# A two-layer diffusion backbone on one core: which engine prepares the operands of the ConvFFN's down projection

## The chip, the core and the metric

The kernel runs on one core of a Trainium2 chip. The core has a matrix engine (TensorE, PE in the profile, with its weight loads as PEld), VectorE (DVE), ScalarE (ACT), GpSimd (POOL) and SyncE (SP), which issues nearly all transfers. Each engine works through its own queue of instructions in order, and semaphores hold an instruction until what it needs is there. The metric is the time of one execution on the device in microseconds; smaller is better.

## What is computed

Two layers act on 1024 latent tokens and 256 context tokens of width 1024. Layer 0 mixes by a Fourier transform and a gated linear attention, layer 1 by grouped-query attention. Each layer ends in a ConvFFN, and the change lies in the last matrix product of these two:

```python
def conv_ffn(h, w_up, w_conv, b_conv, w_down):
    u = dwconv_centred(h @ w_up, w_conv, b_conv)
    g, v = jnp.split(u, 2, axis=-1)
    return (jax.nn.silu(g) * v) @ w_down
...
    h_lat = h_lat + ga2 * conv_ffn(f_lat, w_ffn_up[i], w_ffn_conv[i], b_ffn_conv[i], w_ffn_down[i])
```

The inner width is 2816. Layer 0 puts all 1280 tokens through it, layer 1 the 1024 latent tokens. All is float32.

## The kernel before

**Three products for one.** A float32 operand is split (L206): ScalarE rounds it to the matrix engine's short form (`hi`, the CAST rows of L208), and a subtraction gives the remainder (`lo`, rows of L204). `mm3` then sums lo·hi, hi·lo and hi·hi in PSUM. The subtraction needs `hi`, so it waits for ScalarE. It runs on VectorE, unless another engine is passed in. A row of L204 is thus any two-operand instruction of the helper `tt`: the remainder of a split, a sum or a difference.

**Seven products for eight.** The up and the down projection use a Strassen-like scheme. The weight matrix and the token matrix are cut into 2 by 2 blocks (A11 to A22, B11 to B22), and seven products of block sums give the result. `DOWN` (L1350) lists those of the down projection in their order; the page's rows show them as the matmuls of L154, 128x320 wide in layer 0 and mostly 128x512 wide in layer 1. One product is made of four groups `r` of 128 output columns; a group takes 11 tiles `f` of 128 inner rows, so 33 matmuls for each PSUM bank.

**Weights.** `down_w` (L1424) is a generator that fetches the weight block of product `i`, group `r`, in three pieces of 4, 4 and 3 tiles, that is 512, 512 and 384 columns. Four of the seven products (S1, S3, S2, S4) need a sum of two blocks: two transfers, then a sum in place (L1443) on GpSimd. That makes 48 sums per layer, 32 of 128x512 and 16 of 128x384. The sums S1 and S2 are also stored to DRAM (`sd`, L1454) and loaded again as operands of S2 and S4. Each piece is then split; the table `WE` (L1459) names the engine of the remainder for the three pieces: GpSimd for all three in layer 0, and VectorE, GpSimd, VectorE in layer 1. The pieces lie in ten slots `W`; the generator goes on when a slot is free.

**Tokens.** The class `Ys` (L1359) loads the activations `y` from DRAM in pairs of tiles, forms the block differences that the second, third, fourth and sixth product need (`SUMS`, rows of 128x1280 or 128x1024), and splits each tile `f` of each product `i` (128x640 in layer 0, 128x512 in layer 1). The table `YE` (L1355) names the engine of the remainder: GpSimd for one `f` in three, VectorE for the others. `TE` (L1356) names VectorE for every block difference. A tile's slot `S` is freed when the last group of its product has used it, so most tiles of the next product are made while the last group runs.

**Results.** Each group's PSUM result is added to the residual by VectorE (`resid`, L918), partly by way of L204 rows that read PSUM.

**What sets the order.** The matrix engine's order is written out by hand in both ConvFFNs (L1721, L2052). The order on the other engines is chosen when the kernel is built, by a scheduler that follows the order of the program text and its own estimate of times; `order(first, then)` pins one instruction behind another. In `Ys.conv` a block difference is pinned behind the last split if both are on the same engine.

Of the kernel before, what the change touches and what calls it, by code (L numbers as in the profile page):

```python
# [15 lines left out]
ALU = mybir.AluOpType  # L16
# [88 lines left out]
def tile_hybrid_dit(  # L105
# [12 lines left out]
    V = nc.vector  # L118
    A = nc.scalar
    G = nc.gpsimd  # L120
# [82 lines left out]
    def tt(out_, a, b, op, eng=None):  # L203
        return (eng or V).tensor_tensor(out_, a, b, op)  # L204

    def split(src, hi, lo, eng=None):  # L206

        A.copy(hi, src)  # L208
        return tt(lo, src, hi.bitcast(F32), ALU.subtract, eng)
# [100 lines left out]
    def order(first, then):  # L310

        tc.add_manual_dep(then.ins, first.ins.name, mybir.DependencyInfo(
            mybir.DependencyClass.NoSync, mybir.DependencyReason.DATA), reason="order of the engine")
# [319 lines left out]
    def gla_gates(hf):  # L633

        la = []
        wg = gw[:32, 0, :].rearrange("r (d c) -> r d c", d=2)
        for ct in range(2):
            ab = GM((NT, 256))
            mn = GM((NT, 256))
            for t0, t1 in ((0, 4), (4, 5)):  # L640
                ps = banks(GB, 1024, 2)
                for t in range(t0, t1):
                    c0 = hf * HALF + t * P
                    PE.matmul(ps[:, (t - t0) * 256:(t - t0 + 1) * 256], z_all[:32, c0:c0 + P],
                              wg[:, :, ct * P:(ct + 1) * P], start=True, stop=True)
                pv = ps[:, :(t1 - t0) * 256].rearrange("p (t c) -> p t c", c=256)
                A.activation(ab[:, t0:t1, :], pv, AF.Abs)
                V.tensor_scalar_min(mn[:, t0:t1, :], pv, 0.0)
            A.activation(ab.a, ab.a, AF.Exp, scale=-1.0)
            la.append((ab, mn))  # L650
        for ab, mn in la:
            A.activation(ab.a, ab.a, AF.Ln, bias=1.0)
            tt(ab.a, mn.a, ab.a, ALU.subtract)
            mn.free()
        b = []
        for ct in range(2):
            ab = la[ct][0]
            b.append(GM((2, HALF)))
            for d in range(2):
                ps = banks(GB, HALF, 2)  # L660
                for t in range(NT):
                    PE.matmul(ps[:, t * P:(t + 1) * P], ab[:, t, d * P:(d + 1) * P], gm[:, 7 + d, :],
                              start=True, stop=True)
                A.copy(b[ct][:, d, :], ps)  # L664
            ab.free()
        return b
# [320 lines left out]
    with stream(6):  # L987
        ta, tr = AM(1280), AM(1280)
        R = ta[:, 1024:1280][:, 0:192].rearrange("p (m v b) -> p m v b", m=3, v=2)
# [46 lines left out]
    with stream(1):  # L1036
        b = gla_gates(0)
# [3 lines left out]
    with stream(1):  # L1041
        b = gla_gates(1)
# [309 lines left out]
    KF = NF // 2  # L1352
    LEAVE = (4, 4, 4, 5, 2, 2, 0)
    AHEAD = 3
    YE = ((V, V, G),) * 3 + ((V, G, V),) * 4  # L1355
    TE = (V, V, V, V, V, V, V)  # L1356
    SUMS = {1: ("B11", "B12", "B11"), 2: ("B12", "B22", "B12"), 3: ("B11", "B22", "B11"), 5: ("B11", "B21", "B11")}

    class Ys:  # L1359
# [26 lines left out]
        def conv(self):  # L1386
            i, f = divmod(self.at, KF)
            p, e = divmod(f, 2)
            m = min(2, KF - 2 * p)
            R = lambda b: self.raw[b, p][:, :m]  # L1390
            x = None
            if e == 0 and i in SUMS:
                o, p1, p2 = SUMS[i]
                x = tt(R(o), R(p1), R(p2), ALU.subtract, TE[i])
                if self.last and TE[i] is self.on:
                    order(self.last, x)
            b = ("B11", "B11", "B12", "B11", "B22", "B11", "B21")[i]
            y = S((2, self.n), True)
            ye = YE[i][f % 3]
            self.on = ye  # L1400
            self.last = split(self.raw[b, p][:, e], y[:, 0], y[:, 1], ye)
            self.made[i, f] = y
            if e == m - 1 and i in (2, 4, 5, 6):
                self.raw.pop((b, p)).free()
            self.at += 1
# [18 lines left out]
    def down_w(l, wd):  # L1424

        sd = dr.tile([2, P, 4, KF, P], F32, name=f"sd{l}")

        def src(a, r, f0, m):
            if a in ("S1", "S2"):
                return sd[int(a[1]) - 1, :, r, f0:f0 + m]  # L1430
            j, b = int(a[2]) - 1, (4, 0)[int(a[1]) - 1] + r
            return w_down[l, (j * KF + f0) * P:(j * KF + f0 + m) * P, b * P:(b + 1) * P].rearrange("(f p) c -> p f c", p=P)
        sums = dict(S1=("A21", "A22", ALU.add), S3=("A11", "A21", ALU.subtract), S2=("S1", "A11", ALU.subtract), S4=("A12", "S2", ALU.subtract))
        for i, (a, _) in enumerate(DOWN):
            for r in range(4):
                for f0, m in ((0, 4), (4, 4), (8, 3)) if a in sums else ((0, 8), (8, 3)):
                    if a in sums:
                        raw = W((2, 4, P))
                        for j in range(2):
                            DMA(raw[:, j, :m], src(sums[a][j], r, f0, m))  # L1440
                        yield
                        s = raw[:, 0]
                        tt(s[:, :m], s[:, :m], raw[:, 1, :m], sums[a][2], G)  # L1443
                    else:
                        raw = W((m, P))
                        DMA(raw.a, src(a, r, f0, m))
                        yield
                        s = raw.a
                    for g in range(0, m, 4):
                        k = min(4, m - g)  # L1450
                        wd[i, r, (f0 + g) // 4] = w = W((2, k, P), True)
                        split(s[:, g:g + k], w[:, 0], w[:, 1], WE[l][(f0 + g) // 4])
                        if a in ("S1", "S2"):
                            SD(src(a, r, f0, m), s[:, :m])  # L1454
                        if g + 4 >= m:
                            raw.free()
                        yield
    SD = DMA
    WE = ((G, G, G), (V, G, V))  # L1459

    def ffn(l, n, ups, ops, side, beside, y_d, h_d, after, sides, nsingle, tail, last_groups):

# [2 lines left out]
        ys = Ys(n, y_d)  # L1465
        wd = {}
        w_gen = down_w(l, wd)
        visits = ups.visits
        CU = S.sub(3)
# [641 lines left out]
```

## Time and profile before

| | us |
|---|---|
| median of 3 executions | 3075.54 (3074.51 to 3081.39) |
| the profiled execution | 3070.73 |
| its span, first to last instruction | 3068.9 |

In the profile, a row of the groups names the line, the engine, the operation and the tiles (out<-in, without buffer numbers), the shapes and the count; behind the bar stand the busy time and the mean duration of one instruction, then the engine's idle time just before these instructions and what ended it. A row of the stretches gives, for a stretch of time, each engine's busy time with its count of instructions, the clock that the matrix engine was granted (1.00 is full) and the share of the 16 transfer engines in use. A few records of matmuls may be missing.

### The profile page before, as it was taken

The page shows a single profiled execution, that of the slowest core. Times are in us where ns is not written, and L with a number is a line of the kernel's source. Part 1 is how long each engine was busy: PE and PEld are TensorE (multiplying, and loading weights), DVE is VectorE, ACT ScalarE, POOL GpSimd, SP SyncE. Part 2 cuts the span into 40 slices and gives each one's busy share as a digit, 9 for nine tenths or more (in the row PEclk, how much of TensorE's full clock was granted, in tenths as well). Part 3 has the DMA queues.
Part 4 walks back from the last instruction along what each step waited for, and adds up shares of the span by engine and source line. Part 5 has one row for each costly group of instructions (what it writes and reads, how often), then busy time and mean ns, then how long its engine had stood idle before and what let it go on. Part 6 is the DMA issues. An engine that isn't in the chain of part 4 may idle for free. (4 is left out here: it accounts for less than half of the span.)

```text
span 3068.9 us, 50382 instructions
## 1 busy us (share of the span) xinstructions
PE 2787.4 (91%) x19189; PEld 2612.7 (85%) x19189; DVE 2339.0 (76%) x3891; ACT 1436.7 (47%) x2892; POOL 1225.8 (40%) x1017
## 2 busy tenths in 40 slices
PE   6999988797899999997989899999988999998888
PEld 3899977797889999997989898988967999997667
DVE  7897489869777676767684887877869888887774
ACT  3544433536444444442344545655745544454333
POOL 2025273114332221257884753343344322234661
PEclk7999978998999999998999999999998999999899
DMA  8553302331344433368744220021032222229763
GB/s 277 182 161 96 112 32 89 117 113 62 105 136 127 126 113 122 110 211 268 225 139 132 85 83 26 15 70 59 25 117 69 86 73 77 80 73 283 241 213 109
DMA packets 375784, 371.18 MB, mean 121 GB/s; under 512 B 15579, under 2 KB 305011, under 8 KB 375540
## 3 DMA queue, kind: packets, MB, share of 16 engines
q1 hardware_dynamic: 374482, 365.88, 37.6%
q8 instruction: 151, 2.47, 0.3%
q10 hardware_dynamic: 1058, 2.07, 0.2%
q14 instruction: 93, 0.76, 0.1%
HBM read 282.95 MB, written 84.93 MB: 120 GB/s over the span
## 5 line engine op out<-in xcount | busy, mean ns | idle before, releaser
L154 PE MATMUL psum<-t,t 128*128 128x320 f32 (+4 forms) x17038 | 2592.0, 312 | 194.6 <-DVE t L204 104.1
L154 PEld LDWEIGHTS psum<-t,t 128*128 128x128 f32 x17038 | 2423.8, 194 | 326.4 <-DVE t L204 119.1
L204 POOL TENSOR_TENSOR t<-t,t 128x512 fp32r<-128x512 f32 (+7 forms) x577 | 841.4, 1474 | 897.3 <-ACT t L208 667.6
L204 DVE TENSOR_TENSOR t<-t,t 128x512 fp32r<-128x512 f32 (+12 forms) x919 | 866.3, 973 | 226.1 <-ACT t L208 113.2
L208 ACT CAST t<-t 128x512 fp32r<-128x512 f32 (+5 forms) x857 | 552.4, 671 | 635.2 <-POOL t L204 155.5
L204 POOL TENSOR_TENSOR t<-t 128x320 f32<-128x320 f32 (+2 forms) x216 | 262.8, 1237 | 267.7 <-ACT t L664 155.5
L204 DVE TENSOR_TENSOR t<-t,psum 128x320 f32<-128x320 f32 (+5 forms) x408 | 201.5, 515 | 59.0 <-PE psum L154 36.1
L208 ACT CAST t<-psum 128x512 fp32r<-128x512 f32 (+4 forms) x248 | 130.7, 535 | 135.9 <-PE psum L158 60.3
L1316 POOL COPY halo<-t 128x4 f32<-128x4 f32 x44 | 8.2, 186 | 464.2 <-DVE t L204 453.8
L158 PE MATMUL psum<-ident,t 128*128 128x128 f32 (+2 forms) x955 | 150.7, 280 | 37.2 <-DVE t L204 22.3
L204 DVE TENSOR_TENSOR t<-psum,t 128x512 fp32r<-128x512 f32 (+4 forms) x248 | 151.3, 615 | 38.9 <-ACT t L208 36.3
L1909 POOL TENSOR_SCALAR t<-t,ring 128x640 f32<-128x640 f32 x128 | 101.3, 804 | 170.2 <-DVE ring L1899 80.7
L158 PEld LDWEIGHTS psum<-ident,t 128*128 128x128 f32 (+2 forms) x955 | 113.1, 143 | 46.4 <-DVE t L204 26.3
L1328 ACT ACTIVATE t<-t,cvs 128x639 f32<-128x639 f32 (+3 forms) x176 | 152.0, 864 | 0.0
L918 DVE SCALAR_TENSOR_TENSOR t<-psum,mods,t 128x320 f32<-128x320 f32 (+3 forms) x182 | 87.9, 512 | 61.4 <-PE psum L154 52.1
L1898 DVE TENSOR_REDUCE ring<-psum 128x1 f32<-128x640 f32 x128 | 104.5, 818 | 19.9 <-PE psum L154 15.2
L1327 ACT ACTIVATE t<-t 128x511 f32<-128x511 f32 (+3 forms) x88 | 60.4, 687 | 126.0 <-DVE t L1332 95.4
L1900 ACT ACTIVATE t<-psum,ring 128x640 f32<-128x640 f32 x128 | 102.2, 799 | 25.7 <-DVE ring L1899 12.1
L1300 ACT COPY t<-psum 128x320 f32<-128x320 f32 (+1 forms) x88 | 35.2, 400 | 153.6 <-DVE t L204 102.5
L1336 DVE SCALAR_TENSOR_TENSOR t<-t,cvs,t 128x255 f32<-128x255 f32 (+1 forms) x66 | 54.1, 845 | 66.5 <-ACT t L1328 66.5
L204 DVE TENSOR_TENSOR t<-t 128x128 f32<-128x128 f32 (+3 forms) x167 | 92.9, 583 | 8.2 <-DMA t<-in_w_ffn_up_dram 7.1
L1310 ACT COPY t<-psum 128x320 f32<-128x320 f32 (+1 forms) x88 | 34.9, 397 | 120.5 <-PE psum L154 120.3
(145 smaller groups left out, 1707.3 us busy)
## 6 DMA issues: line engine op xcount, KB each, us to landing
t<-in_w_ffn_up_dram SPq DMA_DIRECT2D x98, 512.0 KB, 4.1
ring<-in_w_mod_dram SPq DMA_DIRECT2D x56, 512.0 KB, 3.9
t<-in_w_ffn_down_dram SPq DMA_DIRECT2D x96, 256.0 KB, 6.0
t<-in_w_even_in_dram SPq DMA_DIRECT2D x28, 512.0 KB, 4.7
t<-in_w_ffn_down_dram SPq DMA_DIRECT2D x72, 192.0 KB, 3.1
t<-y_d SPq DMA_DIRECT2D x20, 640.0 KB, 6.7
t<-in_w_mod_dram SPq DMA_DIRECT2D x96, 128.0 KB, 2.3
t<-in_w_ffn_down_dram SPq DMA_DIRECT2D x24, 512.0 KB, 4.2
```

The source lines that it names most:

```text
L154: cls.keep(out_, nc.tensor.matmul(out_, *args, **kw).ins)
L158: cls.keep(out_, nc.tensor.transpose(out_, *args).ins)
L204: return (eng or V).tensor_tensor(out_, a, b, op)
L208: A.copy(hi, src)
L918: last_resid[0] = V.scalar_tensor_tensor(h[:, n % 2, a:b], ps[:, a - c0:b - c0], mods[:, l, m, n, v:v + 1], h[:, n % 2, a:b], ALU.mult, AL ...
L1300: copied[:] = [A.copy(C(0, 0), ps)]
L1327: order(copied[0], A.activation(us[0], us[0], AF.Silu))
L1328: order(copied[0], A.activation(x, c[:, j, at:at + m], AF.Identity, bias=tap(l, 3, ft), scale=tap(l, 1, ft)))
L1336: V.scalar_tensor_tensor(x[:, s0 + 1:e], c[:, j, 2 + s0:1 + e], tap(l, 0, ft), x[:, s0 + 1:e], ALU.mult, ALU.add)
L1898: V.tensor_reduce(mx[:, i:i + 1], ps, AX.XY, ALU.max)
L1900: A.activation(pt[:, i * HALF:(i + 1) * HALF].rearrange("p (b n) -> p b n", b=2), ps, AF.Exp, bias=nb[:, i:i + 1], scale=SCALE, accum_out= ...
L1909: G.tensor_scalar(pt[:, i * HALF:(i + 1) * HALF], pt[:, i * HALF:(i + 1) * HALF], ex[:, i:i + 1], 1.0, ALU.mult, ALU.mult)
```

## The change

Three places in the code of the down projection change, for both layers:

- `YE` and `TE` go: the remainders of all token tiles and all block differences are on VectorE, and a block difference is always pinned behind the last split.
- The 48 sums of weight blocks per layer go from GpSimd to VectorE.
- In layer 0 the remainder of the third piece of the weights (128x384) goes from GpSimd to VectorE. GpSimd keeps the first two pieces in layer 0 and the middle one in layer 1.

```diff
-    YE = ((V, V, G),) * 3 + ((V, G, V),) * 4
-    TE = (V, V, V, V, V, V, V)
...
-                x = tt(R(o), R(p1), R(p2), ALU.subtract, TE[i])
-                if self.last and TE[i] is self.on:
+                x = tt(R(o), R(p1), R(p2), ALU.subtract)
+                if self.last:
                     order(self.last, x)
...
-            ye = YE[i][f % 3]
-            self.on = ye
-            self.last = split(self.raw[b, p][:, e], y[:, 0], y[:, 1], ye)
+            self.last = split(self.raw[b, p][:, e], y[:, 0], y[:, 1])
...
-                        tt(s[:, :m], s[:, :m], raw[:, 1, :m], sums[a][2], G)
+                        tt(s[:, :m], s[:, :m], raw[:, 1, :m], sums[a][2])
...
-    WE = ((G, G, G), (V, G, V))
+    WE = ((G, G, V), (V, G, V))
```

In all, 174 instructions leave GpSimd's queue and join VectorE's: 89 of 128x512, 25 of 128x640 and 60 of 128x384. The matrix engine's order stays as it was, and the transfers keep theirs but for neighbours that change places. The names below are tiles with their buffer numbers.

**Place A** is in layer 1, at the end of the fourth product (S2, T2), where the matrix engine works on the last group and the tiles of the fifth product are made. On VectorE stood, from the residual rows of the third group to the PSUM row of the last (`t_27196<-t_27196,psum`); rows such as `t_28135<-t_27322,t_28135` are remainders of tokens, `t_28059` and `t_28078` remainders of weights, and the row of 128x1024 is a block difference:

```order
L204 TENSOR_TENSOR t_28135<-t_27322,t_28135 128x512
L204 TENSOR_TENSOR t_28141<-t_27322,t_28141 128x512
L204 TENSOR_TENSOR t_28059<-t_28035,t_28059 128x384
L204 TENSOR_TENSOR t_28150<-t_27398,t_28150 128x512
L204 TENSOR_TENSOR t_28078<-t_28062,t_28078 128x512
L204 TENSOR_TENSOR t_28165<-t_27551,t_28165 128x512
L204 TENSOR_TENSOR t_26818<-t_28153,t_26818 128x1024
L204 TENSOR_TENSOR t_28179<-t_27573,t_28179 128x512
L204 TENSOR_TENSOR t_27196<-t_27196,psum 128x512
```

These are eight rows of two SBUF operands ahead of the PSUM row. In the changed kernel VectorE has at the same place, with the sums of weights as rows that name one tile twice (`t_28097<-t_28097`):

```order
L204 TENSOR_TENSOR t_28132<-t_27296,t_28132 128x512
L204 TENSOR_TENSOR t_28059<-t_28035,t_28059 128x384
L204 TENSOR_TENSOR t_28097<-t_28097 128x384
L204 TENSOR_TENSOR t_28135<-t_27322,t_28135 128x512
L204 TENSOR_TENSOR t_28141<-t_27322,t_28141 128x512
L204 TENSOR_TENSOR t_28144<-t_27398,t_28144 128x512
L204 TENSOR_TENSOR t_28150<-t_27398,t_28150 128x512
L204 TENSOR_TENSOR t_28165<-t_27551,t_28165 128x512
L204 TENSOR_TENSOR t_28078<-t_28062,t_28078 128x512
L204 TENSOR_TENSOR t_28120<-t_28120 128x512
L204 TENSOR_TENSOR t_28171<-t_27551,t_28171 128x512
L204 TENSOR_TENSOR t_28179<-t_27573,t_28179 128x512
```

Twelve rows stand ahead of the PSUM row now: three remainders of tokens and two sums of weights have come in, and the block difference has moved behind it. On GpSimd the same place read, with tokens, sums and remainders of weights (`t_28094`, `t_28032`) in turn:

```order
L204 TENSOR_TENSOR t_28032<-t_28019,t_28032 128x512
L204 TENSOR_TENSOR t_28081<-t_28081 128x512
L204 TENSOR_TENSOR t_28132<-t_27296,t_28132 128x512
L204 TENSOR_TENSOR t_28097<-t_28097 128x384
L204 TENSOR_TENSOR t_28144<-t_27398,t_28144 128x512
L204 TENSOR_TENSOR t_28120<-t_28120 128x512
L204 TENSOR_TENSOR t_28171<-t_27551,t_28171 128x512
L204 TENSOR_TENSOR t_28094<-t_28081,t_28094 128x512
L204 TENSOR_TENSOR t_28201<-t_27588,t_28201 128x512
L204 TENSOR_TENSOR t_28159<-t_28159 128x512
```

Of these ten rows the two remainders of weights stay on GpSimd; its queue there now reads, one row per group of weights:

```order
L204 TENSOR_TENSOR t_27972<-t_27959,t_27972 128x512
L204 TENSOR_TENSOR t_28032<-t_28019,t_28032 128x512
L204 TENSOR_TENSOR t_28094<-t_28081,t_28094 128x512
L204 TENSOR_TENSOR t_28183<-t_28159,t_28183 128x512
L204 TENSOR_TENSOR t_28311<-t_28285,t_28311 128x512
```

The eight other rows have gone to VectorE, where five of them stand in the twelve rows above.

**Place B** is in layer 1, in the second product (S1, T1), whose weights are sums of two blocks from DRAM. On VectorE stood, with the results of a group as `ring<-t_27083,psum` and the residual rows L918 behind it:

```order
L204 TENSOR_TENSOR ring<-t_27083,psum 128x512
L918 SCALAR_TENSOR_TENSOR t_27348<-ring,mods,t_27348 128x512
L918 SCALAR_TENSOR_TENSOR t_27350<-ring,mods,t_27350 128x512
L204 TENSOR_TENSOR t_27365<-t_27342,t_27365 128x384
L204 TENSOR_TENSOR ring<-t_27083,psum 128x512
```

One remainder of weights stands between the results of the two groups. Now the sums `t_27342`, `t_27369` and `t_27389`, each of which waits for its two transfers, stand there too:

```order
L204 TENSOR_TENSOR ring<-t_27083,psum 128x512
L204 TENSOR_TENSOR t_27342<-t_27342 128x384
L918 SCALAR_TENSOR_TENSOR t_27348<-ring,mods,t_27348 128x512
L918 SCALAR_TENSOR_TENSOR t_27350<-ring,mods,t_27350 128x512
L204 TENSOR_TENSOR t_27369<-t_27369 128x512
L204 TENSOR_TENSOR ring<-t_27083,psum 128x512
L204 TENSOR_TENSOR t_27365<-t_27342,t_27365 128x384
L204 TENSOR_TENSOR t_27389<-t_27389 128x512
```

So results that free PSUM banks now stand behind sums that wait for the transfers of weights.

## The prediction

> **What bounds the kernel now.** I read the page first, for the whole; then the stretches of the two down projections, for where the matrix engine stands idle; then the groups by shape, for what fills the engines there; then the order in time of one bad place, and the waits.
>
> ```profile
> span 3068.9 us, 50382 instructions
> PE 2787.4 (91%) x19189; PEld 2612.7 (85%) x19189; DVE 2339.0 (76%) x3891; ACT 1436.7 (47%) x2892; POOL 1225.8 (40%) x1017
> ```
>
> The matrix engine is busy for 91% of the span, so only the places where it isn't can give time back. The change touches only the down projections:
>
> ```profile
> core 0: us, PE busy (x) PEld busy (x) DVE busy (x) ACT busy (x) POOL busy (x), PEclk, DMA share, GB/s
> 1380.00:1440.00 60.00, 50.93 (x327) 49.23 (x326) 40.47 (x42) 16.04 (x28) 46.91 (x33) 0.94 1.01 318
> 1440.00:1600.00 160.00, 137.00 (x846) 132.67 (x847) 124.79 (x133) 58.91 (x95) 135.27 (x86) 0.91 0.58 180
> 2780.00:2866.00 86.00, 77.85 (x335) 61.91 (x333) 67.19 (x70) 30.46 (x56) 51.16 (x33) 0.93 1.00 313
> 2866.00:2998.00 132.00, 107.56 (x412) 82.33 (x411) 98.05 (x101) 50.07 (x90) 86.76 (x60) 0.89 0.61 193
> 2998.00:3058.00 60.00, 60.00 (x354) 52.50 (x352) 26.15 (x68) 18.52 (x35) 7.00 (x6) 1.00 0.36 112
> ...
> 1480.00:1500.00 20.00, 20.00 (x138) 20.00 (x138) 10.91 (x11) 6.41 (x11) 17.43 (x12) 1.00 0.68 202
> 2920.00:2940.00 20.00, 20.00 (x88) 16.23 (x87) 10.18 (x13) 6.26 (x12) 14.43 (x12) 1.00 1.03 336
> ```
>
> The reader sees two kinds of stretch. In 1380 to 1440 (layer 0) and 2780 to 2866 (layer 1) the DMA share is 1.00: transfers are full, a faster helper engine gains nothing there. In 1440 to 1600 and 2866 to 2998 transfers have room, and yet the matrix engine idles and its clock falls to 0.91 and 0.89. The tail (2998 to 3058) is full of matmuls. At its full pace (138 matmuls of layer 0 in 20 us, 0.145 each; 88 of layer 1, 0.227 each) the matrix engine needs 846 x 0.145 = 123 us for the 160, and 412 x 0.227 = 94 for the 132. **The reserve is in these two stretches.**
>
> What VectorE and GpSimd do there:
>
> ```profile
> L154 PE MATMUL psum<-t,t 128*128 128x320 f32 x846 | 137.4, 324 | 24.0 <-DVE t L204 10.1 <-POOL t L204 7.0 <-DVE t L918 4.1
> L204 DVE TENSOR_TENSOR t<-t,t 128x640 fp32r<-128x640 f32 x31 | 50.1, 1639 | 8.4 <-ACT t L208 8.4
> L204 POOL TENSOR_TENSOR t<-t,t 128x512 fp32r<-128x512 f32 x26 | 41.4, 1597 | 7.5 <-ACT t L208 7.5
> L204 POOL TENSOR_TENSOR t<-t,t 128x640 fp32r<-128x640 f32 x17 | 34.2, 2023 | 8.3 <-ACT t L208 5.5 <-DVE t L204 2.8
> L204 POOL TENSOR_TENSOR t<-t 128x512 f32<-128x512 f32 x20 | 31.5, 1578 | 3.1 <-DMA t<-sd 1.9 <-DMA t<-in_w_ffn_down_dram 1.2
> L204 DVE TENSOR_TENSOR t<-t,t 128x1280 f32<-128x1280 f32 x12 | 26.1, 2183 | 0.0
> L204 POOL TENSOR_TENSOR t<-t,t 128x384 fp32r<-128x384 f32 x13 | 17.1, 1313 | 5.8 <-ACT t L208 5.2 <-DMA t<-in_w_ffn_down_dram 0.6
> L204 POOL TENSOR_TENSOR t<-t 128x384 f32<-128x384 f32 x10 | 14.6, 1459 | 0.9 <-DMA t<-in_w_ffn_down_dram 0.9
> ...
> L154 PE MATMUL psum<-t,t 128*128 128x512 f32 x412 | 108.3, 423 | 24.4 <-DVE t L204 15.1 <-ACT t L208 5.2 <-POOL t L204 4.1
> L204 DVE TENSOR_TENSOR t<-t,t 128x512 fp32r<-128x512 f32 x44 | 50.9, 1182 | 11.1 <-ACT t L208 11.1
> L204 POOL TENSOR_TENSOR t<-t,t 128x512 fp32r<-128x512 f32 x31 | 47.8, 1555 | 31.9 <-ACT t L208 31.8
> L204 POOL TENSOR_TENSOR t<-t 128x512 f32<-128x512 f32 x19 | 28.2, 1485 | 7.9 <-DMA t<-in_w_ffn_down_dram 4.4 <-PE psum L154 2.6 <-DMA t<-sd 0.8
> L204 DVE TENSOR_TENSOR t<-t,t 128x1024 f32<-128x1024 f32 x10 | 14.4, 1445 | 0.0
> L204 POOL TENSOR_TENSOR t<-t 128x384 f32<-128x384 f32 x10 | 12.2, 1218 | 5.4 <-DMA t<-in_w_ffn_down_dram 5.2
> L204 DVE TENSOR_TENSOR t<-t,t 128x384 fp32r<-128x384 f32 x14 | 10.9, 781 | 18.6 <-ACT t L208 18.6
> ```
>
> The first eight rows are layer 0, the rest layer 1. Of 24.0 and 24.4 us that the matrix engine idles before matmuls, 21.2 and 19.2 end with a VectorE or GpSimd instruction. And these instructions are slow. The same shapes where the other of the two engines is quiet:
>
> ```profile
> L204 DVE TENSOR_TENSOR t<-t,t 128x512 fp32r<-128x512 f32 x7 | 4.7, 690 | 2.8 <-ACT t L208 2.7
> L204 DVE TENSOR_TENSOR t<-t,t 128x384 fp32r<-128x384 f32 x5 | 2.8, 559 | 9.4 <-ACT t L208 9.4
> L204 POOL TENSOR_TENSOR t<-t,t 128x512 fp32r<-128x512 f32 x6 | 7.7, 1290 | 28.3 <-ACT t L208 28.3
> L204 POOL TENSOR_TENSOR t<-t 128x384 f32<-128x384 f32 x1 | 1.0, 1014 | 0.5 <-PE psum L154 0.5
> 2706.10 1.30 DVE L204 TENSOR_TENSOR t<-t,t 128x512 f32<-128x512 f32 x2 [2.95 <-DMA t<-in_w_ffn_up_dram]
> ```
>
> A 128x512 remainder takes VectorE 0.69 us alone and 1.18 beside GpSimd. Two in a row take 1.30, so the second adds 0.61, which is the price in a full queue (0.47 for 128x384 by the same 0.08 less; 0.76 for 640, 1.22 for 1024 and 1.5 for 1280 columns are estimates in proportion). GpSimd alone takes 1.29 and 1.01 (1.61 for 640, in proportion). Reading PSUM costs VectorE nothing extra beside GpSimd:
>
> ```profile
> L918 DVE SCALAR_TENSOR_TENSOR t<-psum,mods,t 128x512 f32<-128x512 f32 x16 | 11.6, 742 | 1.1 <-PE psum L154 1.1
> L918 DVE SCALAR_TENSOR_TENSOR t<-psum,mods,t 128x512 f32<-128x512 f32 x6 | 4.5, 748 | 3.5 <-PE psum L154 3.5
> ```
>
> The first is of 2866 to 2998, the second of the tail without GpSimd. So two SBUF operands on VectorE and work on GpSimd shut each other out, as if by one access. Adding the own prices, without the waits: layer 0, GpSimd 46 x 1.29 + 17 x 1.61 + 23 x 1.01 = 110, VectorE 31 x 0.76 + 12 x 1.5 = 42, together 152 of 160 us; layer 1, GpSimd 50 x 1.29 + 10 x 1.01 = 75, VectorE 44 x 0.61 + 10 x 1.22 + 14 x 0.47 = 46, together 121 of 132. **This shared access bounds both stretches**, and it is what the change relieves: each instruction that moves needs about half its time there.
>
> **The change part by part.** By the order, 174 instructions move, the matrix engine's row stays. In layer 0's stretch 17 remainders of tokens, 13 of third pieces and 30 sums move: 17 x 0.76 + 23 x 0.47 + 20 x 0.61 = 36 us more for VectorE, and GpSimd keeps 26 x 1.29 = 34 of 110. In layer 1's stretch 14 of the 31 remainders on GpSimd are middle pieces (as many as third pieces on VectorE, 14) and stay, 18 us; 17 and 29 sums move: 17 x 0.61 + 19 x 0.61 + 10 x 0.47 = 27 us.
>
> VectorE's new load: the busy time now, less the waits for the access in the groups above, plus what comes. Layer 0: 124.8 - (76.2 - 42) + 36 = 127 us. Layer 1: 98.1 - (76.2 - 46) + 27 = 95. The matrix engine needs 123 and 94. So the best case is 160 to 127 and 132 to 95, together 70 us; then VectorE and the matrix engine are both full. What remains on GpSimd can still stand in VectorE's way; at worst all of it does, 127 + 34 = 161 and 95 + 18 = 113, which leaves 19 us. The truth lies between 19 and 70. I look at Place A to choose:
>
> ```profile
> 2940.00:2954.00 14.00, 6.62 (x27) 4.15 (x25) 14.00 (x10) 6.28 (x12) 14.00 (x9) 1.00 0.66 208
> 2940.23 13.70 DVE L204 TENSOR_TENSOR t<-t,t 128x512 fp32r<-128x512 f32 x8
> ```
>
> Both helpers are full for 14 us, VectorE does eight rows in 13.7, the matrix engine works for 6.6. The twelve rows of the new order cost 10 x 0.61 + 2 x 0.47 = 7.0 us, and two remainders on GpSimd in the way 2.6: 9.6. The group's 33 matmuls need 7.5. So of 6.5 us lost, 4.4 come back, two thirds. Elsewhere queues are less dense. I take 60% of 70: **-42 us**.
>
> A rule of the Trainium skill speaks for less: "VectorE: DVE Perf Modes", section "The DRAIN you can't avoid", says that the next VectorE operation doesn't start until the pipe of the one before is empty. Then a moved row would cost 0.69 and not 0.61, over the 106 rows of the two stretches 8 us more, and 60% of 62 would be 37. The two instructions in 1.30 us above speak against it here, so the sum stays.
>
> In the full-transfer stretches the added wait counts. A sum waits for its two transfers, and at Place B the rows that free PSUM and the remainders of tokens are queued behind it on VectorE; the matrix engine waits for both.
>
> ```profile
> POOL t L204 <- DMA t<-in_w_ffn_down_dram: 14.6, 9, 3.3
> POOL t L204 <- DMA t<-in_w_ffn_down_dram: 2.0, 2, 1.6
> L154 PE MATMUL psum<-t,t 128*128 128x512 f32 x282 | 72.3, 417 | 8.1 <-DVE t L204 4.1 <-POOL t L204 2.5 <-ACT t L208 1.5
> L154 PE MATMUL psum<-t,t 128*128 128x320 f32 x327 | 51.1, 317 | 8.0 <-POOL t L204 4.1 <-DVE t L204 2.2 <-ACT t L208 1.8
> ```
>
> GpSimd waits 14.6 us (2780 to 2866) and 2.0 (1380 to 1440) for weights today; all of it could reach the matrix engine, +17, or the freer access could remove its idle time there, -16. VectorE is busy for 67 of 86 us, part of that waiting for GpSimd, so a third should get through: **+5**. The added pin of a block difference costs nothing: both rows are on one engine in that order anyway. SyncE's stores of S1 and S2 keep their place and wait for a faster sum. Outside the down projections nothing moves.
>
> Sum: 3070.7 - 42 + 5 = 3033.7 for the profiled execution. The median of the runs is 4.8 higher (3075.5), so 3038.5; I say **3038**.
>
> **The rivals.**
> - VectorE in the way of itself and GpSimd's rest: all 52 us of remaining remainders hold it up. One place speaks for it: `2785.71 6.46`, below, two GpSimd rows in 6.46 instead of 2.6, so the two engines still collide when VectorE is dense. Gain 19 - 5 = 14: 3061.
> - The full gain: both queues run dense, 70 us: 3005 or, with no cost at Place B, a little less. Against it: VectorE waits 11.1 and 18.6 us for ScalarE's casts in layer 1 and still will.
> - Slower: VectorE stands at the sums for weights (Place B and the S2 sums that come back from `sd`). GpSimd waits some 31 us for transfers (24.3 in layer 1, below; in layer 0 the 2.0, and 4.6 in the groups above); if VectorE waits all that and passes it on, against a gain of 19, the time is 3075.5 + 31 - 19 = 3088. It decides from the point where VectorE's waits for transfers that reach the matrix engine exceed the gain. Against it: the weights have ten slots of lead, and a sum costs half.
> - No effect: ScalarE's casts or the transfers take over at once as what is late. ScalarE is busy for 59 of 160 and 50 of 132 us, so little speaks for it: 3073. That the instructions don't move is excluded by the order.
>
> ```profile
> 2785.71 6.46 POOL L204 TENSOR_TENSOR t<-t,t 128x512 fp32r<-128x512 f32 x2 [5.29 <-ACT t L208]
> POOL t L204 <- DMA t<-in_w_ffn_down_dram: 24.3, 17, 3.3
> ```
>
> **How the numbers follow.** Forecast 0.57 (its own range 3022 to 3054), in its own way 0.17, full gain 0.09, slower 0.13, no effect 0.04. A measurement of this kernel tells about 0.2% from no change, 6 us. Faster is the forecast, the full gain and most of the first rival, 0.80; same 0.07; slower 0.13. The range leaves out the worst case and the far end of the best: 3006 to 3074.
>
> **What would show it.** In the profile after, 128x512 and 128x640 remainders on VectorE should take under 0.9 and 1.0 us on average in the late stretches of both stages, GpSimd be busy for under 50 of 160 us there, and the matrix engine's idle time fall from 24 to about 10 in each. Place A should take about 10 us. If VectorE's rows L204 show waits for `in_w_ffn_down_dram` of over 30 us, and the matrix engine idles behind them, the slower rival was right.

## The result and the profile after

The changed kernel takes 3022.27 us (median of 5 runs, 3020.81 to 3035.76); the kernel before, run beside it on the same chip, 3081.39 (3074.51 to 3090.68). The ratio is 0.9832, 95% interval 0.9816 to 0.9849: 1.7% faster, about 52 us. The forecast was 3038 us, 37 less than before; 3022.27 lies within the stated 3006 to 3074, at the very edge of the 3022 to 3054 that the forecast gave itself. The medians of the kernel before differ from call to call (3066 to 3081), so every comparison below is a ratio to the kernel before of the same call, turned into us by that call's median. The profiled execution took 3020.81 us (before 3070.73).

From the page after, the span, then busy time and instruction count of each engine:

```profile
span 3018.9 us, 50383 instructions
PE 2770.2 (92%) x19189; PEld 2601.9 (86%) x19189; DVE 2344.4 (78%) x4065; ACT 1440.7 (48%) x2892; POOL 985.9 (33%) x843
```

VectorE does 174 instructions more than before and is busy for 5 us more (2339.0 before), although the added ones alone would need some 100 (174 at about 0.6, an estimate from the prices of the prediction). So its other instructions became shorter. GpSimd lost 240 us for the same 174.

The stretches of the two down projections, in the profile after, cut at nearly the same matmuls as the stretches that the prediction shows (us; then busy time with the number of instructions per engine, granted clock, DMA share, GB/s):

```profile
core 0: us, PE busy (x) PEld busy (x) DVE busy (x) ACT busy (x) POOL busy (x), PEclk, DMA share, GB/s
1383.00:1435.00 52.00, 48.46 (x328) 47.82 (x326) 41.90 (x65) 15.56 (x28) 17.34 (x10) 1.00 1.06 341
1435.00:1579.00 144.00, 133.02 (x844) 129.38 (x845) 126.69 (x192) 58.69 (x96) 44.61 (x26) 0.93 0.66 207
2749.00:2834.00 85.00, 73.28 (x331) 57.94 (x329) 69.79 (x96) 32.04 (x60) 14.88 (x9) 0.99 1.00 315
2834.00:2948.00 114.00, 104.53 (x413) 80.21 (x414) 96.30 (x143) 48.13 (x87) 26.00 (x14) 0.94 0.71 224
2948.00:3008.00 60.00, 59.94 (x352) 52.33 (x350) 28.55 (x72) 19.27 (x37) 7.03 (x5) 1.00 0.36 113
```

All four stretches became shorter, also those with full transfers. The tail is unchanged. In layer 1 the rows can't be subtracted as they stand: the prediction's cut at 2866 lies ahead of a stop of 4.7 us, which ends with the matmul at 2871.2, and the cut at 2834 behind nearly all of the like stop after. The table below cuts behind the stop in both. The groups by shape in the two late stretches after (count, busy us, mean ns, idle time before them with what ended it), layer 0 first:

```profile
L154 PE MATMUL psum<-t,t 128*128 128x320 f32 x844 | 133.3, 320 | 13.4 <-DVE t L204 9.1 <-ACT t L208 4.3
L204 POOL TENSOR_TENSOR t<-t,t 128x512 fp32r<-128x512 f32 x26 | 44.6, 1722 | 95.4 <-ACT t L208 93.8 <-DVE t L204 1.6
L204 DVE TENSOR_TENSOR t<-t,t 128x640 fp32r<-128x640 f32 x48 | 42.3, 912 | 2.9 <-ACT t L208 2.9
L204 DVE TENSOR_TENSOR t<-t,t 128x1280 f32<-128x1280 f32 x12 | 18.9, 1573 | 0.0
...
L154 PE MATMUL psum<-t,t 128*128 128x512 f32 x411 | 104.5, 413 | 14.4 <-ACT t L208 8.8 <-DVE t L204 5.5
L204 DVE TENSOR_TENSOR t<-t,t 128x512 fp32r<-128x512 f32 x58 | 41.3, 741 | 2.6 <-ACT t L208 2.6
L204 POOL TENSOR_TENSOR t<-t,t 128x512 fp32r<-128x512 f32 x14 | 27.9, 1993 | 89.4 <-ACT t L208 66.2 <-DMA t<-h_d 8.9 <-PE psum L154 5.1
```

VectorE's token remainders fell from 1639 to 912 ns in layer 0, and its 128x512 remainders (tokens and first pieces of weights) from 1182 to 741 in layer 1. In these two stretches the matrix engine no longer waits for GpSimd, and its idle time fell from 24.0 to 13.4 and from 24.4 to 14.4 us.

Every kernel here has 19189 matmuls, and in the down projections they stand in the same order, so the k-th of one trace can be held against the k-th of another. Outside, the program built is not always the same: by the shapes of the matmuls some kernels differ in up to 30 places, and tokens_alone in 742, between 1872 and 2059 of the profile before. The table gives what each profile gained on the profile before between the same matmuls (those that start at 1380.1, 1441.2, 1600.2, 2780.1, 2871.2 and 2998.0 us before), in us; "rest" is the remainder of the execution. The kernels of the other rows are explained in the next section.

| kernel | layer 0, full transfers | layer 0, late | layer 1, full transfers | layer 1, late | rest |
|---|---|---|---|---|---|
| changed kernel | 9.1 | 14.8 | 5.2 | 13.7 | 7.5 |
| before, a second profile | -2.0 | 0.6 | 1.0 | 1.1 | -3.3 |
| tokens_alone | 5.7 | 4.6 | 1.7 | 7.5 | 14.3 |
| sums_alone | 3.8 | 6.9 | 3.1 | 8.1 | -1.0 |
| third_alone | 2.6 | 5.4 | 1.5 | 0.7 | 0.8 |
| sums_back | 4.9 | 6.3 | 3.2 | 7.6 | 12.0 |
| before_slot | -7.7 | -2.7 | -6.1 | 0.0 | 2.2 |
| slot_control | -2.5 | 2.3 | 0.1 | 4.9 | 11.9 |
| shadow | -9.3 | -24.5 | -7.8 | -6.4 | -3.1 |
| shadow_copy | -5.1 | -4.3 | -4.3 | 1.0 | 7.9 |
| no_gpsimd | 12.4 | 19.1 | 6.7 | 7.8 | 16.6 |
| vvv0 | 12.2 | 19.3 | 5.7 | 12.3 | 7.0 |
| vvv0_lead | 13.4 | 20.9 | 6.5 | 12.3 | 9.9 |

The second profile of the kernel before shows how far such rows can be trusted: about 2 us in a stretch. The rest scatters between -3 and 17 us. It is 7 to 17 in the kernels that have all token remainders on VectorE, shadow alone excepted, and -3 to 2 in the others, so it need not be chance; but it is spread over the span in pieces of under 5 us, and no cause was traced. So what the change does in the down projections is read from this table, and the ratios are totals that have the rest in them.

### The profile page after: what moved, and what is told of

Read it like the earlier page. It is cut to its first block, busy times and chain, and to the rows that moved or that the text cites. A ratio compares the mean times of both kernels' runs of the same rounds, so it can differ in the third digit from the quotient of the medians.

```text
span 3018.9 us, 50383 instructions
## 1 busy us (share of the span) xinstructions
PE 2770.2 (92%) x19189; PEld 2601.9 (86%) x19189; DVE 2344.4 (78%) x4065; ACT 1440.7 (48%) x2892; POOL 985.9 (33%) x843
## 5 line engine op out<-in xcount | busy, mean ns | idle before, releaser
L204 POOL TENSOR_TENSOR t<-t,t 128x512 fp32r<-128x512 f32 (+8 forms) x499 | 736.4, 1492 | 1124.7 <-ACT t L208 856.9
L204 DVE TENSOR_TENSOR t<-t,t 128x512 fp32r<-128x512 f32 (+12 forms) x997 | 829.5, 863 | 195.2 <-ACT t L208 87.0
L204 DVE TENSOR_TENSOR t<-t 128x512 f32<-128x512 f32 (+3 forms) x263 | 164.8, 646 | 45.4 <-DMA t<-in_w_ffn_down_dram 31.7
L204 POOL TENSOR_TENSOR t<-t 128x320 f32<-128x320 f32 (+2 forms) x120 | 124.0, 1067 | 225.0 <-ACT t L664 157.2
L918 DVE SCALAR_TENSOR_TENSOR t<-psum,mods,t 128x320 f32<-128x320 f32 (+3 forms) x182 | 88.3, 513 | 42.7 <-PE psum L154 39.8
L1894 DVE TENSOR_REDUCE ring<-psum 128x1 f32<-128x640 f32 x128 | 104.5, 818 | 19.4 <-PE psum L154 13.6
```

The costliest lines, as they stand in the source:

```text
L918: last_resid[0] = V.scalar_tensor_tensor(h[:, n % 2, a:b], ps[:, a - c0:b - c0], mods[:, l, m, n, v:v + 1], h[:, n % 2, a:b], ALU.mult, AL ...
L1894: V.tensor_reduce(mx[:, i:i + 1], ps, AX.XY, ALU.max)
```

## The experiments

Theories when they began. **A**: VectorE instructions with two SBUF operands and GpSimd work shut each other out, and the change relieves that shared access. **B**: GpSimd's one queue is late, whatever it shares; any part that unblocks it gives most of the gain. **C**: the sums cost VectorE as much waiting as they bring. **D**: GpSimd is merely slow, and the two engines do not hinder each other.

**The parts of the change, each alone, and one undone.**

```diff
tokens_alone (from before)
-    YE = ((V, V, G),) * 3 + ((V, G, V),) * 4
+    YE = ((V, V, V),) * 7
sums_alone (from before)
-                        tt(s[:, :m], s[:, :m], raw[:, 1, :m], sums[a][2], G)
+                        tt(s[:, :m], s[:, :m], raw[:, 1, :m], sums[a][2])
third_alone (from before)
-    WE = ((G, G, G), (V, G, V))
+    WE = ((G, G, V), (V, G, V))
sums_back (from the changed kernel)
-                        tt(s[:, :m], s[:, :m], raw[:, 1, :m], sums[a][2])
+                        tt(s[:, :m], s[:, :m], raw[:, 1, :m], sums[a][2], G)
```

> Only the token splits go to VectorE; the sums and all weight splits of before stay on GpSimd. Theory A (shared access: each instruction moved frees about 0.7 us of an access that is full, so the parts add up in proportion to what they move; of the 50 us, 39 of 115 us of freed access are tokens): about 17 us less than before. Theory B (the lateness of GpSimd's one queue: remainders that the matrix engine waits for stand behind sums that wait for transfers; any part that unblocks the queue gives most of the gain, and the parts do not add): 35 to 45 us less. Theory C (sums on VectorE cost as much as they bring, tokens and third pieces carry the gain): 50 us less or more.

Measured: 0.9899 (0.9879 to 0.9919), 31 us less than before.

> Only the sums of weights go to VectorE. Theory A: 61 of 115 us of freed access, about 26 us less than before. Theory B: GpSimd's queue no longer waits for two transfers per sum, 35 to 45 us less. Theory C: VectorE stands at the sums, within 10 us of before or slower.

Measured: 0.9940 (0.9920 to 0.9960), 18 us less.

> Only the third piece of each weight in layer 0 goes to VectorE. Theory A: 15 of 115 us of freed access, about 7 us less than before, all of it in layer 0. Theory B: under 5 us, since the sums and the token splits stay in GpSimd's queue. Theory C: says nothing of it.

Measured: 0.9981 (0.9967 to 0.9994), 6 us less.

> The changed kernel with its sums back on GpSimd (token splits and third pieces stay on VectorE). Theory A: about 24 us less than before, 26 more than the changed kernel. Theory B: tokens no longer stand behind the sums, 40 to 50 us less than before. Theory C: VectorE no longer waits for transfers, over 50 us less than before, faster than the changed kernel.

Measured: 0.9899 (0.9880 to 0.9917), 31 us less.

By the totals the three parts add up: 31 + 18 + 6 = 55, against 52 for all. By the four stretches of the table tokens_alone gains 19.5 us, sums_alone 21.9 and third_alone 10.2, together 51.6 against 42.8 for all, so the parts overlap a little, if the difference is more than noise.

Both counts are against B, in which each of the first two would have given 35 or more alone: the 31 of tokens_alone has 14.3 of the rest in it. Both are against C: the sums bring 18 alone and 52 - 31 = 21 on top of the others, in the stretches 21.9 and 42.8 - 22.0 = 20.8. A's proportions missed in the totals, where tokens brought more than the 17 expected and sums less than 26; in the stretches, where A acts, 19.5, 21.9 and 10.2 are near its 17, 26 and 7.

The late stretches of tokens_alone (layer 0, then layer 1):

```profile
L154 PE MATMUL psum<-t,t 128*128 128x320 f32 x846 | 137.0, 324 | 19.1 <-DVE t L204 15.3 <-ACT t L208 3.8
L204 DVE TENSOR_TENSOR t<-t,t 128x640 fp32r<-128x640 f32 x48 | 57.2, 1226 | 9.6 <-ACT t L208 9.6
...
L154 PE MATMUL psum<-t,t 128*128 128x512 f32 x410 | 107.2, 421 | 16.8 <-DVE t L204 9.5 <-ACT t L208 7.3
```

No wait of the matrix engine for GpSimd is left; before, it waited 7.0 and 4.1 us for it here, and 4.1 and 2.5 in the full-transfer stretches, 17.7 together (of the full-transfer stretches of tokens_alone, 0.4 is left). Token remainders are what the matrix engine waits for directly. But the idle time fell only from 24.0 to 19.1 and from 24.4 to 16.8 us, since in layer 0 the waits for VectorE rose from 10.1 to 15.3. Whether theory B adds something to this part beside the access is not shown.

**The access itself.** `shadow` puts the load back on GpSimd, but with nobody waiting for its results. It needs a place to write, so one of the 31 token buffers is set aside; `slot_control` sets it aside and does nothing with it.

```diff
slot_control (from the changed kernel)
+    shade = [None]
...
         S.join(CU)
+        shade[0] = S((2, n))
...
+            if i == 6:
+                shade.pop(0).free()
+                shade.append(None)
shadow (from slot_control)
+    def shadow(hi):
+        if shade[0]:
...
+            tt(o.rearrange("p (k c) -> p k c", c=P), h, h, ALU.subtract, G)
...
             self.made[i, f] = y
+            if f % 3 == (2 if i < 3 else 1):
+                shadow(y[:, 0])
...
+                        if a in sums:
+                            shadow(w[:, 0])
+                        if not l and f0 + g == 8:
+                            shadow(w[:, 0])
shadow_copy (from shadow)
-            tt(o.rearrange("p (k c) -> p k c", c=P), h, h, ALU.subtract, G)
+            G.tensor_copy(o.rearrange("p (k c) -> p k c", c=P), h)
```

> The changed kernel with one of the 31 token buffers set aside, unused, in the first six products of each down projection: the control of the next run. All theories: the loads of tokens run one buffer less ahead, 0 to 8 us more than the changed kernel, so 42 to 52 us less than before.

Measured: 0.9953 (0.9937 to 0.9970), only 14 us less than before: the missing buffer took 37 of the 52. That much was not expected, and before_slot, below, follows it up.

> The control with 174 extra GpSimd subtractions less those before the buffer is there, one for each instruction that the change took from GpSimd and of its shape. They read the rounded half that ScalarE wrote and write to the buffer set aside; nothing waits for their result, and the output is unchanged. Theory A (two SBUF operands on VectorE and GpSimd work exclude each other): the 128x512 remainders of VectorE take 1.1 us or more on average in the late stretches again (0.7 in the control's quiet places) and most of the gain is lost: 35 us or more above the control. Theory D (GpSimd merely is slow at work that is waited for, and the two do not hinder each other): the extra work is hidden, within 6 us of the control.

Measured: 1.0147 (1.0123 to 1.0171), 45 us slower than before and 1.94% or 59 us above the control. 164 instructions were added, which keep GpSimd busy for 207 us. The matmuls and the token remainders in layer 0's late stretch, by shape, of the control:

```profile
L154 PE MATMUL psum<-t,t 128*128 128x320 f32 x844 | 138.3, 327 | 18.0 <-DVE t L204 12.6 <-ACT t L208 5.3
L204 DVE TENSOR_TENSOR t<-t,t 128x640 fp32r<-128x640 f32 x49 | 42.8, 903 | 1.6 <-ACT t L208 1.4
```

and the same with the shadows:

```profile
L154 PE MATMUL psum<-t,t 128*128 128x320 f32 x843 | 146.5, 336 | 37.9 <-DVE t L204 30.4 <-ACT t L208 7.4
L204 DVE TENSOR_TENSOR t<-t,t 128x640 fp32r<-128x640 f32 x47 | 57.9, 1262 | 1.7 <-ACT t L208 1.6
```

VectorE's rows are the same instructions in both, and nothing waits for the results of the added ones, yet each remainder takes 1262 instead of 903 ns and the matrix engine waits 30.4 instead of 12.6 us for VectorE. D falls and A is shown. Layer 1's 128x512 remainders rose too, less than to the 1.1 us expected (control, then shadows):

```profile
L204 DVE TENSOR_TENSOR t<-t,t 128x512 fp32r<-128x512 f32 x57 | 41.0, 746 | 6.3 <-ACT t L208 5.9
L204 DVE TENSOR_TENSOR t<-t,t 128x512 fp32r<-128x512 f32 x57 | 54.0, 976 | 3.4 <-ACT t L208 3.1
```

One other path is open to the added work: a buffer that it reads comes free only behind it. It is the smaller one: over the four stretches ScalarE waits 39.4 us for GpSimd instead of 31.8. And the 59 us are no measure of A's share in the gain: here VectorE does the moved work as well, so both engines together do more than before the change.

The Trainium skill has such a rule in "SBUF — State Buffer", section "SBUF: two separate sides": a VectorE operation with two SBUF inputs and a GpSimd operation that reads SBUF hold one port pair in turns, each for its whole instruction. The trace agrees in the direction, and in that reads of PSUM beside GpSimd cost nothing extra, as layer 0's late stretch has it in the control and with the shadows:

```profile
L918 DVE SCALAR_TENSOR_TENSOR t<-psum,mods,t 128x320 f32<-128x320 f32 x18 | 9.6, 542 | 0.0
L918 DVE SCALAR_TENSOR_TENSOR t<-psum,mods,t 128x320 f32<-128x320 f32 x17 | 9.0, 538 | 0.0
```

> As the run with the extra GpSimd subtractions, but each is a copy (one operand read where the subtraction reads two), of the same shape and at the same place. Theory A, by time on GpSimd whatever it does there: if a copy takes as long as a subtraction, as much above the control, 45 us or more. If only the reading of two operands holds the access: under 15 us above the control.

Measured: 1.0021 (1.0007 to 1.0035), 0.68% or 21 us above the control: over the 15 of the second outcome, and short of the 40 that the first would give for the copies' time (59 x 138/207). The rows of layer 0's late stretch:

```profile
L204 DVE TENSOR_TENSOR t<-t,t 128x640 fp32r<-128x640 f32 x49 | 48.9, 1027 | 2.9 <-ACT t L208 2.9
L1365 POOL COPY t<-t 128x512 f32<-128x512 f32 x20 | 18.8, 938 | 0.7
L1365 POOL COPY t<-t 128x640 f32<-128x640 f32 x15 | 17.8, 1189 | 2.8 <-ACT t L208 2.3
```

A copy takes 938 ns where the subtraction took 1454 (128x512), and slows VectorE less: 1027 ns. GpSimd is busy for 138 us more than in the control (1120.0 against 982.0), so per us of GpSimd time a copy costs 21/138 = 0.15 us of the kernel, the subtraction 59/207 = 0.29. So a GpSimd instruction with one operand holds VectorE up as well, but about half as much for its time. Why is open.

**The missing buffer.** Does the control lose because the buffer is gone, or because the change needs it?

```diff
before_slot (from before): as slot_control
         S.join(CU)
+        shade[0] = S((2, n))
```

> The kernel before with one of the 31 token buffers set aside, unused, in the first six products of each down projection, as in the control, which lost 37 of the change's 52 us. Theory L (the missing buffer costs what it costs, whoever does the splits: token loads run later): 25 to 40 us more than before. Theory M (the change gains by giving buffers back sooner, so that loads run ahead; the kernel before, with GpSimd late, never used that lead): within 10 us of before.

Measured: 1.0054 (1.0038 to 1.0069), 17 us slower than before: between the two. With one buffer fewer the change gains 0.9953 against 1.0054, 31 us; with all of them 52. By the four stretches it is 4.8 + 16.5 = 21 against 43. So by either count some 20 us of the gain depend on the buffer, the part that theory M named, and the rest do not. The shadows, at 1.0147, are 28 us above this kernel. Layer 0's full-transfer stretch in the control, as a window:

```profile
1383.00:1447.00 64.00, 51.27 (x328) 49.93 (x326) 44.54 (x68) 15.84 (x28) 16.14 (x9) 0.92 0.87 274
```

its group of matmuls:

```profile
L154 PE MATMUL psum<-t,t 128*128 128x320 f32 x328 | 51.6, 319 | 12.7 <-ACT t L208 11.3 <-DVE t L204 1.3
```

and the same group in the changed kernel:

```profile
L154 PE MATMUL psum<-t,t 128*128 128x320 f32 x328 | 48.7, 310 | 1.1 <-DVE t L204 1.1
```

With 30 buffers the transfers are no longer full (0.87 for 1.06), the matrix engine stands 11.3 us for casts, and the stretch lasts 64 us instead of 52. The issues of the token loads agree. Held against the matmuls (by the start, in the profile before, of the next matmul after each issue), the four that go out between 1368 and 1395 in the profile before go out 3.4, 4.1, 6.6 and 6.6 us earlier in the changed kernel; in the control the first of them is 9.4 us later than in the changed kernel, the others 0 to 3.

**Less on GpSimd still.**

```diff
no_gpsimd (from the changed kernel)
-    WE = ((G, G, V), (V, G, V))
+    WE = ((V, V, V), (V, V, V))
vvv0 (from the changed kernel)
-    WE = ((G, G, V), (V, G, V))
+    WE = ((V, V, V), (V, G, V))
vvv0_lead (from vvv0)
-    LEAVE = (4, 4, 4, 5, 2, 2, 0)
+    LEAVE = (3, 3, 3, 4, 2, 2, 0)
```

> The changed kernel with all weight splits on VectorE in both layers, no GpSimd work left in the down projections but the norms'. Theory A: what GpSimd held of the access goes, and its rows cost half on VectorE; VectorE's own load rises to 143 us in layer 0's late stretch, which took 145, so about 5 to 15 us less than the changed kernel if the access still binds, and 0 to 10 more if VectorE itself does. Theory D: VectorE, the busiest helper, takes 16 + 9 us more in the late stretches, 10 to 25 us more than the changed kernel.

Measured: 0.9817 (0.9798 to 0.9837), 56 us less than before, about 5 less than the changed kernel; the intervals overlap. The 10 to 25 us more that D forecast did not come.

> Layer 0 without GpSimd splits, layer 1 as in the changed kernel (its middle weight pieces on GpSimd). The profiles of the run without GpSimd gained about 8 us more than the changed kernel in layer 0 and 4 less in layer 1. If the two layers are independent: 5 to 10 us less than the changed kernel, 3 to 6 less than without GpSimd. If the difference between the profiles is chance: within 3 us of both.

Measured: 0.9813 (0.9794 to 0.9833), 57 us less than before, 6 less than the changed kernel, with overlapping intervals, and not to be told from no_gpsimd. By the table no_gpsimd gains 8 us more than the changed kernel in layer 0 and 4 less in layer 1, vvv0 keeps both good halves, but that difference is too small for the runs. Layer 0's late stretch in vvv0, as a window and then its token remainders:

```profile
1437.00:1577.00 140.00, 129.96 (x848) 126.76 (x849) 129.80 (x222) 60.06 (x98) 0.00 (x0) 0.96 0.69 217
```

```profile
L204 DVE TENSOR_TENSOR t<-t,t 128x640 fp32r<-128x640 f32 x48 | 38.0, 819 | 0.6 <-ACT t L208 0.6
```

Without GpSimd a 128x640 remainder takes 819 ns, and VectorE, busy for 129.8 of 140 us, is now as full as the matrix engine.

> The run above with one idle token buffer fewer left over in the first four products (LEAVE 3, 3, 3, 4 for 4, 4, 4, 5), so that loads and splits of tokens run one buffer further ahead. Theory L: the reverse of the control, 5 to 20 us less than the run above. If the loads of the residual stream need the idle buffers: 0 to 20 us more.

Measured: 0.9812 (0.9792 to 0.9832), the same as vvv0. A buffer taken away costs 37 us, but this edit gains nothing that can be told from noise. That the lead is long enough is not shown by it: of the loads just named, the first goes out 4.1 us later than in vvv0, the others within 1.4 us of it, so in this stretch the loads did not run further ahead.

**The noise.**

> The kernel before once more, for a second profile: how far one profile's stretches outside the down projections differ from another's with nothing changed. All theories: under 2 us in each stretch of the down projections, and up to 6 elsewhere.

Measured: one more profile, the second row of the table above. It lies within 2.1 us of the first in each of the four stretches, and 3.3 apart elsewhere.

## Why the prediction came out as it did

**The mechanism was right, and is shown.** Work on GpSimd makes VectorE's rows longer and the matrix engine wait (shadow). After the change VectorE's rows got shorter (912 and 741 ns, under the 1.0 and 0.9 us that were asked for), GpSimd is busy for 44.6 us in layer 0's late stretch (under 50 asked for), and the new load of VectorE, worked out as 127 and 95 us, was measured as 126.7 and 96.3. In layer 0 that agreement is partly luck: the five groups that the working prices at 78 us took 91.8 by their rows, some 83 without the overlap of 0.08 us a row, while rows that it held fixed became shorter (`t<-t,ring` of 128x640 from 10.8 to 6.3 us). The prices of full queues held too; after the change two rows follow each other on VectorE like this:

```profile
2828.26 0.55 DVE L204 TENSOR_TENSOR t<-t,t 128x384 fp32r<-128x384 f32 x1
2828.73 0.68 DVE L204 TENSOR_TENSOR t<-t 128x512 f32<-128x512 f32 x1
```

From start to start the 128x384 remainder takes 0.47 us, as estimated, and the second begins before the first has ended. The rule that was weighed, of "VectorE: DVE Perf Modes", section "The DRAIN you can't avoid" in the Trainium skill, would have the second start after 0.55; but that section also says "A next op that is not held starts earlier", and these rows agree with that.

**Two terms were mis-sized, in opposite directions.**

*The late stretches: -42 forecast, 14.8 + 13.7 = 28.5 us measured.* The step that failed is "I take 60% of 70", in two ways. First, Place A was no sample of the whole. It did better than forecast: its 13.9 us, from the matmul at 2940.09 to the one at 2953.99, became 5.6, where the working gave 9.6. (24 matmuls start in it, not the group's 33 that the working took, so 13.9 - 24 x 0.227 = 8.4 us were lost there, and 8.3 came back.) The matrix engine runs through it without a stop (the timeline after):

```profile
2895.82 12.88 PE L154 MATMUL psum<-t,t 128*128 128x512 f32 x55
2910.51 1.66 PE L154 MATMUL psum<-t,t 128*128 128x512 f32 x6 [1.81 <-DVE t L204]
```

But of the other losses in the two stretches, 48.4 us idle and 28.7 above the best pace less these 8.4, only 28.5 - 8.3 = 20.2 of 68.7 came back. Between 2885 and 2940 before, where the matrix engine ran nearly without a stop, nothing did (-1.2 us between the same matmuls). A densely filled place was chosen because its loss was plain to see, and its share was carried to places where less could be had. Second, the 70 counted matmuls at their best pace, 123 and 94 us. They were busy for 133.3 and 104.5: of the 48.4 us of idle time 20.6 came back, but of the 28.7 us above the best pace (137.4 + 108.3 - 217) only 7.9, with the granted clock at 0.93 and 0.94.

*The full-transfer stretches: +5 forecast, 9.1 + 5.2 = 14.3 us gained.* The step that failed is the sentence at the very start, that where transfers are full "a faster helper engine gains nothing there". Here even the end of the range that was given for the freer access (-16) was nearly reached. The transfers were full because they ran ahead; what the matrix engine waited for were remainders, and the faster splits gave buffers back sooner, so the loads ran further ahead still: by 3 to 7 us in layer 0, as told above, where the DMA share went from 1.01 to 1.06. In layer 1 the like four loads go out only 0.3 to 2.6 us earlier, and the gain there, 5.2 us, was not traced as far. The control with one buffer fewer shows what happens when the loads can't run ahead.

**The wait for the sums came, and cost next to nothing.** The group on the page after that holds the sums (and other rows of their form):

```profile
L204 DVE TENSOR_TENSOR t<-t 128x512 f32<-128x512 f32 (+3 forms) x263 | 164.8, 646 | 45.4 <-DMA t<-in_w_ffn_down_dram 31.7
```

and the waits in the two full-transfer stretches after, layer 1's first (engine, line and what it waited for: us, times, longest):

```profile
DVE t L204 <- DMA t<-in_w_ffn_down_dram: 11.0, 9, 3.0
PE psum L154 <- DVE t L204: 2.1, 4, 1.0
...
DVE t L204 <- DMA t<-in_w_ffn_down_dram: 6.9, 5, 3.5
PE psum L154 <- DVE t L204: 1.1, 1, 1.1
```

VectorE waits 31.7 us, which is over the 30 that the slower rival asked for, but its second condition failed: in these two stretches, where 17.9 of the 31.7 lie, the matrix engine waits 3.2 us for VectorE. VectorE had room there (69.8 of 85 us busy), so a wait is taken from its idle time. sums_alone gained in both stretches. In the two late stretches VectorE waits another 10.5 us for weights, and how much of the 14.6 us that the matrix engine waits for VectorE there goes back to them was not traced; sums_alone gained there too.

**The other rivals.** GpSimd's rest does collide with a dense VectorE (1993 ns for a remainder of layer 1 that takes 1290 alone), but by the waits it holds up the matrix engine directly for only 1.8 us, in layer 1's full-transfer stretch. What it costs by way of VectorE, no_gpsimd and vvv0 tell, which take it away: 5 to 6 us, within the noise of the runs. So the first rival's price did not come due. The full gain did not come either: VectorE was busy for 126.7 of 144 and 96.3 of 114 us, and what is late next is now visible. The longest stop left stands at the border of layer 1's two stretches and is the first below (the timelines of the matrix engine and of VectorE after, in order: start, us, row, and the idle time before it):

```profile
2834.48 0.79 PE L154 MATMUL psum<-t,t 128*128 128x512 f32 x1 [5.44 <-ACT t L208]
```

```profile
2831.71 2.48 DVE L204 TENSOR_TENSOR t<-t,t 128x1024 f32<-128x1024 f32 x2 [0.19 <-DMA t<-y_d]
```

A block difference of tokens on VectorE follows the landing of its load from `y_d`, the cast follows the difference, and the matmul the cast. VectorE stood idle for only 0.19 us before the difference, so the load was hardly later than VectorE's own queue.

**The sum.** 28.5 + 14.3 = 42.8 us in the four stretches, against 42 - 5 = 37 forecast: two errors of 14 and 19 us that nearly cancelled. That the total came so near was luck. The other 7.5 us of this profile lie outside the four stretches, where the change moves only a few instructions, at the edges of the down projections; since a second profile of the same kernel differs there by 3.3, and other kernels by up to 17, whether any of it belongs to the change stays open.

## What to carry to other kernels

A helper engine that isn't waited for can still be the bound, if it holds what another engine needs. Here it paid to have subtractions and sums of SBUF data on VectorE rather than beside it on GpSimd, as long as VectorE had room. Such a suspicion can be tested with extra work whose results nobody waits for. Full transfers don't mean that transfers are late; look at what the matmuls wait for in that stretch, and at how many buffers of lead the loads have. A recovery rate read from one bad place must be weighted by how many such places there are. And the whole program is built anew for each small edit: see whether it differs elsewhere before a part's gain is read from a total.

## What the runs showed of the hardware that was not expected

- GpSimd's own rows get longer beside a dense VectorE: its 128x512 remainder took 1290 ns in the tail, where VectorE is less busy, 1555 before and 1993 after the change in layer 1's late stretch, with fewer of them.
- A GpSimd copy (one operand) slows VectorE about half as much per us as a subtraction: 0.15 against 0.29 us of the kernel.
- The granted clock in layer 0's late stretch is lowest where the matrix engine idles most and highest where it idles least: 0.86 with 37.9 us idle (shadow), 0.91 with 24.0 (before), 0.93 with 13.4 (after), 0.96 with 11.0 (vvv0). In between the order is loose: 0.88 with 23.3 (shadow_copy), 0.89 with 18.0 (slot_control), 0.94 with 19.7 (sums_alone). That idle time lowers the clock was not tested.
